# Twenty gate weight jobs as seven block products each, with branch results, gates and head outputs parked in DRAM

## The chip, the cores and the metric

The kernel runs on one core of a Trainium2 chip. Its engines are TensorE (PE, with its weight loads as PEld), VectorE (DVE), ScalarE (ACT), GpSimd (POOL) and SyncE (SP), which issues nearly all DMAs. The metric is device time in microseconds of one execution, as the median of several.

## The reference

One layer of a streaming encoder over 512 prompt tokens and 64 sample tokens (576 columns in the kernel), width 1024. One input projection feeds three branches; a gate of each branch and a merge gate come out of the same projection.

```python
xn = rms_norm(x, g_norm)
hq, hf, hi, za, dq, dk, dv, zb, mq, zm, gr = split_columns(xn @ w_in)
...
y_a = rms_norm(o_hg.transpose(0, 2, 1, 3), g_hg_out).reshape(B, T, HG_WIDTH)
...
y_b = (rms_norm(o_df, g_dsub) * (1.0 - lam_init)).reshape(B, T, DF_WIDTH)
...
y_m = memory_attention(q_m, mem_k, mem_v).reshape(B, T, MEM_WIDTH)

gates = jax.nn.sigmoid(gr).reshape(B, T, N_BRANCH, D_MODEL)
h = 0
for n, (y_n, z_n) in enumerate(((y_a, za), (y_b, zb), (y_m, zm))):
    h = h + gates[:, :, n] * ((y_n * jax.nn.silu(z_n)) @ w_branch[n])
y = x + h @ w_out
```

Branch a is a gated recurrence over 8 heads, b a differential attention over 8 heads, m an attention over 256 memory tokens with 4 heads, whose keys and values come from `rms_norm(mem_prompt) @ w_mkv`. The caches of keys, values and states are outputs too.

## The kernel before

**Arithmetic.** All products of projections are made to nearly full float32 precision from a rounded "hi" part and a "lo" remainder of each operand: hi·hi, hi·lo and lo·hi, so three matmuls for each block of 128 x 128 weights. The normalised input lies in SBUF as `xh` and `xl`, transposed. Weights come from DRAM as `raw` halves of 512 KB (`load_job`, line 163, through SP), ACT copies each quarter to `wh` (line 174), and DVE and POOL in turn make `wl` as raw minus `wh` (line 176, `lo_engine`).

**Jobs.** 76 jobs of 1024 x 256 weights each run on PE in the order of a list. A "T" job puts weights in the array and gives two blocks of 128 output channels by two halves of 288 tokens: four groups of 24 matmuls (line 213), 96 in all. An "N" job gives tokens by channels in matmuls of 256 columns (line 245): 96 over the 512 prompt tokens and 16 for the sample rows (line 257), or 48 over the 256 memory tokens. `mms` is a generator that stops after every 12 matmuls or so; at each stop `run_jobs` (line 314) converts some of the next job's weights and `weave` (line 294) takes a tick: it runs what `later` put off to this tick, and lets each active generator go one step. The work between projections (the recurrence `hgrn`, `diff_pair`, `mem_head`, the norms) is such generators, so PE's projections are the cover under which DVE, ACT and POOL do the rest. The order on each engine is this program order; nothing reorders it.

**The list.** Four recurrence pairs (hi, za, hf, hq), four jobs gr0 of branch a's merge gate, four br0 (`w_branch[0]`), the sixteen memory jobs (query, zm, key, value for each head), four gr2 and four br2, four attention pairs (dq, dk, dv, zb), four gr1 and four br1, four output jobs. The work of the last pair of each branch lies under the gr jobs that follow it.

**Evacuation.** A gr job's result is one Tanh on ACT per half (line 1356) into a `gates` tile. A z job adds one DVE operation per half (line 476, after ACT's line 475). A branch job multiplies the gate with PE's result and adds it to the running sum `h2` (lines 1368 to 1372), which stays in SBUF.

**The gates of the branch jobs.** Each finished head output is split at once into hi (ACT, line 459) and lo (POOL, line 462, `y_out`). The first branch job multiplies three groups over heads 0 to 5 (54 matmuls), then waits in the program until no generator is active, opens its `gate`, and does heads 6 and 7. SBUF scratch is a pool of "slots" (line 42): 33, and 14 more once the recurrence's own memory is given back.

Of the kernel before, what the change touches and what calls it, by code (L numbers as in the profile page):

```python
# [36 lines left out]
CW = 256  # L37

# [26 lines left out]
def encoder_step(ctx, tc, ins, outs):  # L65
# [10 lines left out]
    raws = pool("raws", 3)  # L76
    whls = pool("whls", 4)
# [32 lines left out]

    def sample_rows(key, w=CW, n=2, rows=HS0):

        ts = srows.setdefault(key, [])
        if len(ts) < n:
            ts.append(cst.tile([P, w], F32, name=nm("pad" + key)))
# [16 lines left out]
    NBASE = 33  # L132
    NMORE = 14
# [18 lines left out]
    class Job:  # L152
        def __init__(self, src, c0, kind, evac, name, pre=None, lhs=None):
            self.src, self.c0, self.kind, self.evac, self.name, self.pre, self.lhs = src, c0, kind, evac, name, pre, lhs
            self.raw, self.hi, self.lo, self.gate, self.last, self.up = [], None, None, None, False, False
# [7 lines left out]
    def load_job(j, parts=(0, 1)):  # L163
        for kh in parts:
            r = raws.tile([P, 4, CW], F32, tag="raw", name=nm("raw"))
            sy.dma_start(out=r, in_=j.src[:, 4 * kh : 4 * kh + 4, j.c0 : j.c0 + CW])
            j.raw.append(r)

    def conv_job(j, now=False):

        j.hi, j.lo, out = [], [], []

        def split(hi, lo, src):
            se.activation(out=hi, in_=src, func=AF.Copy)  # L174
            e = lo_engine()
            fn = lambda: e.tensor_tensor(out=lo, in0=src, in1=hi.bitcast(F32), op=ALU.subtract)  # L176
            if now:
                fn()
            else:
                later(1, fn)  # L180
        if j.kind == "T":
            def conv(blk, kh):
                if kh == 0:
                    j.hi.append(whls.tile([P, NK, P], F32R, tag="wh", name=nm("wh")))
                    j.lo.append(whls.tile([P, NK, P], F32R, tag="wl", name=nm("wl")))
                src = j.raw[kh][:, :, blk * P : (blk + 1) * P]
                split(j.hi[blk][:, 4 * kh : 4 * kh + 4, :], j.lo[blk][:, 4 * kh : 4 * kh + 4, :], src)
            for kh in range(2):
                for blk in range(2):
                    out.append(lambda blk=blk, kh=kh: conv(blk, kh))  # L190
        else:
            def conv(kh, s):
                if s == 0:
                    j.hi.append(whls.tile([P, 4, CW], F32R, tag="wh", name=nm("wh")))
                    j.lo.append(whls.tile([P, 4, CW], F32R, tag="wl", name=nm("wl")))
                src = j.raw[kh][:, 2 * s : 2 * s + 2, :]
                split(j.hi[kh][:, 2 * s : 2 * s + 2, :], j.lo[kh][:, 2 * s : 2 * s + 2, :], src)
            for kh in range(2):
                for s in range(2):
                    out.append(lambda kh=kh, s=s: conv(kh, s))  # L200
        return out

    def mms(j):

        if j.kind == "T":
            hi, lo = j.lhs()

            def group(blk, half, ps, k0, k1):
                sl = slice(half * TH, (half + 1) * TH)
                n = 3 * k0  # L210
                for k in range(k0, k1):
                    for w, x in ((j.hi, hi), (j.hi, lo), (j.lo, hi)):
                        pe.matmul(out=ps[:, 0:TH], lhsT=w[blk][:, k, :], rhs=x(k)[:, sl], start=(n == 0), stop=(n == 23))  # L213
                        n += 1
                        if n == 12:
                            yield
                if k1 == NK:
                    later(1, lambda: j.evac(blk, half, ps[:, 0:TH]))
                yield
            groups = [(blk, half) for blk in range(2) for half in range(2)]  # L220
            if j.gate:

                early = [(blk, half, dbank()) for blk, half in groups[0:3]]
                for g in early:
                    yield from group(*g, 0, 6)
                while active:
                    yield
                j.gate()
                for g in early:
                    yield from group(*g, 6, NK)  # L230
                groups = groups[3:]
            for blk, half in groups:
                yield from group(blk, half, dbank(), 0, NK)
        else:
            hi, lo, st, ntok = j.lhs()
            w = lambda ws, k: ws[k // 4][:, k % 4, :]

            def prompt(t2):
                ps = dbank()
                for t in range(2):  # L240
                    sl = slice((2 * t2 + t) * P, (2 * t2 + t + 1) * P)
                    n = 0
                    for k in range(NK):
                        for x, ww in ((hi, j.hi), (hi, j.lo), (lo, j.hi)):
                            pe.matmul(out=ps[:, t * CW : (t + 1) * CW], lhsT=x(k)[:, sl], rhs=w(ww, k), start=(n == 0), stop=(n == 23))  # L245
# [6 lines left out]
            def sample():  # L252
                ps = dbank()
                n = 0
                for k in range(NK):
                    for ww in (j.hi, j.lo):
                        pe.matmul(out=ps[:, 0:CW], lhsT=st[:, k, :], rhs=w(ww, k), start=(n == 0), stop=(n == 15))  # L257
# [11 lines left out]
            if st is not None and not j.last:  # L269
                yield from sample()  # L270

# [40 lines left out]
    jobs = []  # L312

    def run_jobs():
        n = len(jobs)
        for i, j in enumerate(jobs):
            if j.pre:
                j.pre()
            convs = deque(conv_job(jobs[i + 1])) if i + 1 < n else deque()

            def convert():
                convs.popleft()()
                if len(convs) % 2 == 0 and i + 2 < n:
                    later(1, lambda kh=1 - len(convs) // 2: load_job(jobs[i + 2], (kh,)))
            for s, _ in enumerate(mms(j)):
                if convs and (i or s >= 4) and len(jobs[i + 1].raw) > (4 - len(convs)) // 2:
                    convert()
                weave()
            while convs:
                convert()  # L330
# [125 lines left out]
    def y_out(h, tmp):  # L456

        hi, lo = yT[h] = slots.get(F32R), slots.get(F32R)
# [1114 lines left out]
```

## Time and profile before

| | |
|---|---|
| median of 3 runs | 1127.91 us (1127.91 to 1129.07) |
| the profiled execution's own time | 1130.34 us |
| its span in the trace | 1128.3 us |
| mean granted TensorE clock | 0.997 |
| PE busy, matmuls | 1110.9 us, 8925 |
| DVE busy | 624.2 us |
| ACT busy | 470.5 us |
| POOL busy | 461.3 us |
| DMA | 102.13 MB, mean 91 GB/s |

A row of the groups reads: line, engine, operation, output from inputs, tile shapes and count; then busy time, mean duration in ns, and the idle time of the engine just before, with what ended it. A row of the chain of waits or of the timeline begins with the start in us and the duration; "xN" is the number of instructions in it, and a bracket tells how long the engine had been idle and what released it. A row of the windows gives, for a stretch of time, the busy us and the instruction count of PE, PEld, DVE, ACT and POOL, then the granted clock, the DMA engines' busy share and GB/s.

### The profile page before, as it was taken

The page shows a single profiled execution, that of the slowest core. Times are in us where ns is not written, and L with a number is a line of the kernel's source. Part 1 is how long each engine was busy: PE and PEld are TensorE (multiplying, and loading weights), DVE is VectorE, ACT ScalarE, POOL GpSimd, SP SyncE. Part 2 cuts the span into 40 slices and gives each one's busy share as a digit, 9 for nine tenths or more (in the row PEclk, how much of TensorE's full clock was granted, in tenths as well). Part 3 has the DMA queues.
Part 4 walks back from the last instruction along what each step waited for, and adds up shares of the span by engine and source line. Part 5 has one row for each costly group of instructions (what it writes and reads, how often), then busy time and mean ns, then how long its engine had stood idle before and what let it go on. Part 6 is the DMA issues. An engine that isn't in the chain of part 4 may idle for free.

```text
span 1128.3 us, 22032 instructions
## 1 busy us (share of the span) xinstructions
PE 1110.9 (98%) x8925; PEld 1098.7 (97%) x8925; DVE 624.2 (55%) x1223; ACT 470.5 (42%) x1103; POOL 461.3 (41%) x590
## 2 busy tenths in 40 slices
PE   7999999999999999999999999999999998999998
PEld 6999999999999999999999999999999998999998
DVE  5459594967733345443422323578686785654531
ACT  6433333343341355444433213465565664653320
POOL 2436455555442154525221554436363563232120
PEclk9999999999999999999999999999999999999999
DMA  5322222122133245334221232414113123112242
GB/s 188 113 80 66 81 63 84 58 85 76 62 118 98 73 141 152 93 114 150 76 67 56 76 96 64 149 54 136 44 61 126 58 77 97 38 59 92 96 137 68
DMA packets 103093, 102.13 MB, mean 91 GB/s; under 512 B 4914, under 2 KB 101326, under 8 KB 102992
## 3 DMA queue, kind: packets, MB, share of 16 engines
q1 hardware_dynamic: 102988, 100.73, 28.7%
q8 instruction: 70, 1.15, 0.4%
q14 instruction: 31, 0.25, 0.1%
q10 hardware_dynamic: 4, 0.00, 0.0%
HBM read 90.49 MB, written 10.22 MB: 89 GB/s over the span
## 4 chain that ended last, share of the span: by engine, by line
PE 91%; DVE 4%; DMA 2%; POOL 1%; issue 1%; ACT 1%; SPq 0%; DVEq 0%; POOLq 0%
PE d L213 49%; PE d L245 25%; PE d L257 4%; PE abank L1023 1%; DMA raw<-in_w_in_dram 1%; PE abank L1226 1%; PE abank L1293 1%; PE abank L990 1%; PE abank L688 1%; PE abank L952 1%; PE abank L724 1%; PE abank L745 1%; PE abank L544 1%; DVE wl L176 1%; PE abank L951 1%
## 5 line engine op out<-in xcount | busy, mean ns | idle before, releaser
L176 POOL TENSOR_TENSOR wl<-raw,wh 128x512 fp32r<-128x512 f32 x152 | 208.3, 1374 | 348.4 <-ACT wh L174 347.5
L213 PE MATMUL d<-xh,wh 128*128 128x288 f32 x1024 | 310.8, 304 | 0.0
L213 PE MATMUL d<-xh,wl 128*128 128x288 f32 x1024 | 302.6, 295 | 0.0
L213 PE MATMUL d<-xl,wh 128*128 128x288 f32 x1024 | 302.5, 295 | 0.0
L245 PE MATMUL d<-wh,xh 128*128 128x256 f32 x768 | 221.9, 289 | 1.5 <-ACT xh L435 1.5
L245 PE MATMUL d<-wh,xl 128*128 128x256 f32 x768 | 218.0, 284 | 0.2 <-DVE xl L438 0.2
L174 ACT ACTIVATE wh<-raw 128x512 fp32r<-128x512 f32 x304 | 181.7, 623 | 87.1 <-PE d L213 61.7
L245 PE MATMUL d<-wl,xh 128*128 128x256 f32 x768 | 217.7, 283 | 0.0
L213 PEld LDWEIGHTS d<-xh,wh 128*128 128x128 f32 x1024 | 193.5, 189 | 1.0
L213 PEld LDWEIGHTS d<-xl,wh 128*128 128x128 f32 x1024 | 193.4, 189 | 0.4
L213 PEld LDWEIGHTS d<-xh,wl 128*128 128x128 f32 x1024 | 193.1, 189 | 0.0
L176 DVE TENSOR_TENSOR wl<-raw,wh 128x512 fp32r<-128x512 f32 x152 | 121.4, 799 | 123.2 <-ACT wh L174 121.2
L213 PE MATMUL d<-slot,wh 128*128 128x288 f32 x768 | 153.5, 296 | 0.0
L245 PEld LDWEIGHTS d<-wh,xh 128*128 128x128 f32 x768 | 147.4, 192 | 2.2 <-ACT xh L435 1.9
L245 PEld LDWEIGHTS d<-wh,xl 128*128 128x128 f32 x768 | 147.4, 192 | 0.7 <-DVE xl L438 0.7
L245 PEld LDWEIGHTS d<-wl,xh 128*128 128x128 f32 x768 | 147.6, 192 | 0.3
L213 PEld LDWEIGHTS d<-slot,wh 128*128 128x128 f32 x768 | 123.2, 188 | 0.0
L213 PE MATMUL d<-slot,wl 128*128 128x288 f32 x384 | 113.3, 295 | 0.0
L213 PEld LDWEIGHTS d<-slot,wl 128*128 128x128 f32 x384 | 72.3, 188 | 0.0
L1356 ACT ACTIVATE slot<-d 128x288 f32<-128x288 f32 x48 | 19.8, 412 | 107.0 <-PE d L213 107.0
L475 ACT ACTIVATE slot<-d 128x288 f32<-128x288 f32 x48 | 19.5, 409 | 92.8 <-PE d L213 91.0
L462 POOL TENSOR_TENSOR slot<-slot,slot 128x576 fp32r<-128x576 f32 x24 | 35.3, 1472 | 54.5 <-ACT slot L459 54.5
(283 smaller groups left out, 1853.1 us busy)
## 6 DMA issues: line engine op xcount, KB each, us to landing
raw<-in_w_in_dram SPq DMA_DIRECT2D x104, 512.0 KB
raw<-in_w_branch_dram SPq DMA_DIRECT2D x24, 512.0 KB
raw<-in_w_mkv_dram SPq DMA_DIRECT2D x16, 512.0 KB
out_dram<-slot SPq DMA_DIRECT2D x31, 256.0 KB
slot<-in_x_prompt_dram SPq DMA_DIRECT2D x16, 256.0 KB
raw<-in_w_out_dram SPq DMA_DIRECT2D x8, 512.0 KB
slot<-in_mem_prompt_dram SPq DMA_DIRECT2D x4, 256.0 KB
slot<-in_cache_mem_k_dram SPq DMA_DIRECT2D x4, 256.0 KB
```

The lines of the kernel that those rows point to most:

```text
L174: se.activation(out=hi, in_=src, func=AF.Copy)
L176: fn = lambda: e.tensor_tensor(out=lo, in0=src, in1=hi.bitcast(F32), op=ALU.subtract)
L213: pe.matmul(out=ps[:, 0:TH], lhsT=w[blk][:, k, :], rhs=x(k)[:, sl], start=(n == 0), stop=(n == 23))
L245: pe.matmul(out=ps[:, t * CW : (t + 1) * CW], lhsT=x(k)[:, sl], rhs=w(ww, k), start=(n == 0), stop=(n == 23))
L257: pe.matmul(out=ps[:, 0:CW], lhsT=st[:, k, :], rhs=w(ww, k), start=(n == 0), stop=(n == 15))
L462: ge.tensor_tensor(out=lo[:, 0:TT], in0=tmp[:, 0:TT], in1=hi[:, 0:TT].bitcast(F32), op=ALU.subtract)
L475: se.activation(out=dst, in_=ps, func=AF.Tanh, scale=0.5)
L544: pe.transpose(pt[:, c * P : (c + 1) * P], on[:, c * P : (c + 1) * P], ident)
L688: pe.matmul(out=a1[o0 : o0 + 64, (c % NT) * P + 32 * i : (c % NT) * P + 32 * i + 32], lhsT=Kb[:, c * KP + i * P + r0 : c * KP + i * P + r0 ...
L724: pe.matmul(out=a4[:, c * P : (c + 1) * P], lhsT=kET[:, c * P : (c + 1) * P], rhs=vt(c), start=True, stop=True)
L745: pe.matmul(out=ob[:, c * P : (c + 1) * P], lhsT=aS[:, c * P : (c + 1) * P], rhs=vt(c), start=True, stop=(c == 0))
L1356: se.activation(out=gates[b][:, half * TH : (half + 1) * TH], in_=ps, func=AF.Tanh, scale=0.5)
```

## The change

**Seven products.** A new job kind "S" is used for zb, zm and all gr jobs: 20 jobs. It takes the weights as 2 x 2 blocks (half of the depth by 128 channels) and the input as 2 x 2 blocks (half of the tokens by half of the depth) and forms the result from 7 block products of 12 matmuls, in the Winograd form, where a T job has 8. The sums of weights are made per job; the sums of the input, S1 to S4 with their hi and lo, once in `build_XS` during br0. za stays "T", since it runs before that. These are the weight sums and the seven products; `split` makes a hi on ACT and a lo on the engine named.

```python
            def op_t2(now):
                t1 = add("t1", part(0, 0), part(0, 1), ve)
                t2 = add("t2", sums["t1"], part(1, 1), ve)
...
                split(sums["t2"], P, None, now, ve, 1)
            def op_b21(now):
                split(part(1, 0), P, 1, now, ge)
                t4 = add("t4", sums["t2"], part(1, 0), ge)
...
            def op_t3(now):
                t3 = add("t3", part(0, 1), part(1, 1), ge)
...
                split(sums["t3"], P, None, now, ve, 1, t3)
            ops.append((i, 0, lambda now: split(part(0, 0), P, 0, now, ge)))
...
        order = (("A11", 0, 1), ("S2", 1, 1), ("A12", 0, 0), ("S3", 1, 0), ("S1", 2, 1), ("A22", 1, 0), ("S4", 2, 0))
...
            if p == 0:
                later(1, lambda ps=ps: se.activation(out=u1, in_=ps, func=AF.Copy))
            elif p == 1:
                later(1, lambda ps=ps: ve.tensor_tensor(out=u2, in0=ps, in1=u1, op=ALU.add))
            elif p == 2:
                later(1, lambda ps=ps: j.evac(0, 0, ps))
            elif p == 3:
                later(1, lambda ps=ps: ve.tensor_tensor(out=u3, in0=ps, in1=u1, op=ALU.add))
            elif p == 4:
                later(1, lambda ps=ps: finish(1, 1, c22, ps, u3, True))
            elif p == 5:
                later(1, lambda ps=ps: finish(0, 1, c21, ps, u1, False))
            else:
                later(1, lambda ps=ps: finish(1, 0, c12, ps, u2, True))
```

The second entry of `order` is the PSUM bank, the third whether the product starts a sum in it. A bank keeps adding after `u1`, `u2`, `u3` were read from it, so each of these reads comes between two products of its bank: u1 before product 2, u2 before product 3, u3 before product 5, and each `finish` before its bank's next use.

The listings below name instructions as line, operation, output from inputs and shape.

On DVE, at the third gr2 job of before (wl and raw are weight parts; L1190, L1234, L1247 and L1248 belong to the memory attention of the last head):

```order
L1300 SCALAR_TENSOR_TENSOR slot4_220_5917<-abank2_81,slot4_220_5917 128x512
L1300 SCALAR_TENSOR_TENSOR slot12_223_6022<-abank0_79,slot12_223_6022 128x512
L176 TENSOR_TENSOR wl_546_6832<-raw_539_6687,wh_545_6831 128x512
L1190 SCALAR_TENSOR_TENSOR slot13_264_6759<-abank3_82,gmq_103,slot35_262_6757 128x512
L176 TENSOR_TENSOR wl_546_6832<-raw_541_6723,wh_545_6831 128x512
L1190 SCALAR_TENSOR_TENSOR slot17_265_6760<-abank4_83,gmq_103,slot20_263_6758 128x512
L1234 TENSOR_REDUCE mx1_554_6949<-abank0_79 128x1
L176 TENSOR_TENSOR wl_558_6979<-raw_549_6859,wh_557_6978 128x512
```

On DVE, at the third gr2 job of after (L247 makes weight sums, L216 a lo, L435 and L437 finish an output block, d is a bank of the job's products, the others belong to attention heads):

```order
L247 TENSOR_TENSOR slot30_330_7425<-raw_755_7187 128x512
L247 TENSOR_TENSOR slot1_331_7427<-slot30_330_7425,raw_767_7268 128x512
L1461 TENSOR_REDUCE mx1_783_7410<-abank1_82 128x1
L435 SCALAR_TENSOR_TENSOR slot15_332_7432<-d_785_7412,slot8_189_4872 128x288
L1474 RECIPROCAL zz1_777_7356<-zz1_777_7356 128x1
L1475 TENSOR_SCALAR slot14_329_7398<-slot14_329_7398,zz1_777_7356 128x256
L1029 TENSOR_TENSOR slot20_304_6991<-slot20_304_6991,rsn256_764_7249 128x512
L216 TENSOR_TENSOR wl_787_7430<-slot1_331_7427,wh_786_7429 128x512
L437 TENSOR_TENSOR slot17_328_7376<-d_773_7324,slot9_188_4871 128x288
```

Where two subtractions per job stood on DVE, there are now two sums, four subtractions, and five operations that read a product bank, in one queue with the heads' work.

**The list.** The eight memory key and value jobs run right after the recurrence's jobs, in the place of gr0; their results go to DRAM (lines 1342 and 1357) and are loaded again for the heads (line 1367). gr0 comes after br0, gr2 is spread between the memory heads, and br2 lies inside the first attention pair, between dv and zb.

**Parking.** Head outputs 0 to 5 of each branch are stored to DRAM (line 647), loaded again one at a time, and split then (`y_splits`, line 654, ACT for hi and POOL for lo); 6 and 7 are split from SBUF. Branch results and gates go to DRAM and back (`h_store`, `h_load`, `g_store`, `g_load`, lines 1579 to 1595). The slots are 32 throughout; the recurrence's memory becomes the tile `XS`.

```python
            while h not in yF or len(slots.free) < (12 if hurry[0] == 1 else 4 if hurry[0] else NSPARE):
                yield
            tmp = yF.pop(h)
            if tmp is None:
                tmp = slots.get()
                sy.dma_start(out=tmp[:, 0:TT], in_=y_d[h])
                for _ in range(2 if hurry[0] else 4):
                    yield
```

**The branch gates.** The first job of br0, br1, br2 now multiplies as many heads as are split at that point, 4 to 6 (`y_there`), and then takes empty ticks until all eight are.

```python
-                    yield from group(*g, 0, 6)
-                while active:
+                    yield from group(*g, 0, k0)
+                while len(yT) < 8:
                     yield
```

In br0 and br1, k0 comes out as 4, so each of the three early groups has 12 matmuls, and six empty ticks follow; in br2 no empty tick is taken.

On SP, at br1 of before, only weight halves stand (raw):

```order
L166 DMA raw_943_11644<-in_w_in_dram 128x4x256
L166 DMA raw_960_11839<-in_w_branch_dram 128x4x256
L166 DMA raw_968_11905<-in_w_branch_dram 128x4x256
L166 DMA raw_981_12075<-in_w_branch_dram 128x4x256
L166 DMA raw_985_12118<-in_w_branch_dram 128x4x256
```

On SP, at br1 of after (y_ are parked head outputs, h2_ and g1_ parked branch results and gates):

```order
L662 DMA slot16_677_12904<-y_3_111 128x576
L185 DMA raw_1363_12946<-in_w_branch_dram 128x4x256
L1584 DMA slot15_682_12955<-h2_0_142 128x576
L1593 DMA slot28_683_12957<-g1_0_150 128x576
L1584 DMA slot5_684_12959<-h2_1_143 128x576
L1593 DMA slot18_685_12961<-g1_1_151 128x576
L1584 DMA slot3_686_12963<-h2_2_144 128x576
L1593 DMA slot27_687_12965<-g1_2_152 128x576
L1588 DMA g1_6_156<-slot22_672_12840 128x576
L185 DMA raw_1369_12993<-in_w_branch_dram 128x4x256
L1588 DMA g1_7_157<-slot17_676_12901 128x576
L662 DMA slot24_688_12997<-y_4_112 128x576
```

Six loads of parked results and two stores of gates now stand between the loads of head outputs 3 and 4 in this queue.

**Weights.** `load_next`, `conv_next` and `plan` take the place of `load_job` and `conv_job`: eight quarter units of converted weights, whatever the job, where there were four half units.

More of the change, by code (lines that the diff above doesn't have):

```diff
@@ L161, in lo_engine @@
         return ge if lo_n[0] % 2 == 0 else ve
[L163 to L176, printed above, removed]
+    jobs = []
@@ new lines, in encoder_step, with load_next @@
+    halves = []
+    units = []
+    ops = deque()
+    def load_next(limit):
+        n = len(halves)
+        i, kh = n // 2, n % 2
+        if i >= min(len(jobs), limit) or (n >= NRAW and halves[n - NRAW][2]):
+            return False
+        j = jobs[i]
+        r = raws.tile([P, 4, CW], F32, tag="raw", name=nm("raw"))
+        sy.dma_start(out=r, in_=j.src[:, 4 * kh : 4 * kh + 4, j.c0 : j.c0 + CW])
+        j.raw.append(r)
+        halves.append([j, kh, j.readers[kh]])
+        return True
@@ new lines, in conv_next, with plan, read, split @@
+    def conv_next(limit, now=False):
+        if not ops or ops[0][0] >= limit or len(jobs[ops[0][0]].raw) <= ops[0][1]:
+            return False
+        if len(units) >= NUNIT and not units[-NUNIT].done:
+            return False
+        ops.popleft()[2](now)
+        return True
+    def plan(i, j):
+        j.units = []
+        base = 2 * i
+        def read(kh):
+            halves[base + kh][2] -= 1
+        def split(src, width, kh, now, eng=None, wait=0, free=None):
+            u = Unit(width)
+            units.append(u)
+            j.units.append(u)
+            def fhi():
+                se.activation(out=u.hi, in_=src, func=AF.Copy)
+            def flo():
+                (eng or lo_engine()).tensor_tensor(out=u.lo, in0=src, in1=u.hi.bitcast(F32), op=ALU.subtract)
+                if free:
+                    slots.put(free)
+                if kh is not None:
+                    read(kh)
@@ L188, in conv_job @@
+            for blk in range(2):
+                for kh in range(2):
+                    ops.append((i, kh, lambda now, blk=blk, kh=kh: split(j.raw[kh][:, :, blk * P : (blk + 1) * P], P, kh, now)))
+        elif j.kind == "N":
+            j.readers = [2, 2]
             for kh in range(2):
-                for blk in range(2):
-                    out.append(lambda blk=blk, kh=kh: conv(blk, kh))
-        else:
[L192 to L200, printed above, removed]
@@ L206, in mms, with unit, done @@
+    def mms(j):
+        def unit(n):
+            while len(j.units) <= n:
+                assert conv_next(len(jobs)), (j.name, n)
+            return j.units[n]
+        def done():
+            for u in j.units:
+                u.done = True
+        if j.kind == "S":
+            yield from strassen(j, unit)
+        elif j.kind == "T":
             hi, lo = j.lhs()
@@ L1449, in end_hgrn, with y_start, y_next, y_all @@
             weave()
+        slots.put(*mT.values())
         hstack.close()
         more = ctx.enter_context(tc.tile_pool(name="more", bufs=1))
[L1452 to L1457 removed]
+        XS.append(more.tile([P, 2, 4, 4, TH], F32R, name="XS"))
+        push(build_XS(), 1.0)
+    def y_start():
+        hurry[0] = 0
+        push(y_splits(), 1.0)
+    def y_next():
+        y_free()
+        y_start()
+    js = branch_jobs(0)
     js[0].gate = end_hgrn
     seq += js
[L1461 to L1465 removed]
+    js = gr_jobs(0)
+    before(js[0], y_next)
+    seq += js
+    def y_all():
+        pass
     MA = []
+    gr = gr_jobs(2)
     for h in range(4):
@@ L1498, in encoder_step @@
     before(js[0], drain)
+    before(js[0], lambda: y_free())
     seq += js
     jobs.extend(seq)
+    for i, j in enumerate(jobs):
+        plan(i, j)
     with tc.manual_schedule():
```

399 lines of the change are left out of this document (291 added, 108 removed).

## The prediction

> **What bounds the kernel now.** I read the page's busy times and its chain first.
>
> ```profile
> PE 1110.9 (98%) x8925; PEld 1098.7 (97%) x8925; DVE 624.2 (55%) x1223; ACT 470.5 (42%) x1103; POOL 461.3 (41%) x590
> ...
> PE 91%; DVE 4%; DMA 2%; POOL 1%; issue 1%; ACT 1%; SPq 0%; DVEq 0%; POOLq 0%
> ```
>
> PE is busy for 98% of the span and carries 91% of the chain of waits. Time falls only if PE gets less to do, and rises by each wait on PE that is new. So the price of PE's work comes next, from the chain in the stages where nothing interrupts a job: one T job, one N job, and 12 matmuls of a T job.
>
> ```profile
> 1008.09 12.72 PE d L213 x96
> 1070.61 11.52 PE d L245 x96
> 942.60 1.59 PE d L213 x12
> ```
>
> A T job is 96 matmuls in 12.72 us, 132.5 ns each; 12 of them, one product, are 1.59 us. An N job is 120 ns each. The averages of DVE (55%) and POOL (41%) say little: they are spread over stages with different loads, and the windows below show that.
>
> **PE's saving.** Each of 20 jobs issues 84 matmuls for 96, of the same size (128 x 128 weights, 288 columns). 20 x 12 = 240 fewer, times 132.5 ns, is **−31.8 us**. All of it is on the path, since PE is. A seven-product job needs 84 x 132.5 ns = 11.13 us of PE.
>
> **What the seven products ask of the other engines.** The rows for their parts are the weight splits and the operations that read a PSUM bank:
>
> ```profile
> L176 DVE TENSOR_TENSOR wl<-raw,wh x152: 666/692/1955, 8.4 to 1099.5; 128x512 fp32r<-128x512 f32 x152
> L176 POOL TENSOR_TENSOR wl<-raw,wh x152: 1265/1292/2059, 9.0 to 1100.5; 128x512 fp32r<-128x512 f32 x152
> ...
> L174 ACT ACTIVATE wh<-raw 128x512 fp32r<-128x512 f32 x304 | 181.7, 623 | 87.1 <-PE d L213 61.7
> L476 DVE SCALAR_TENSOR_TENSOR slot<-slot,d 128x288 f32<-128x288 f32 x48 | 21.7, 453 | 55.6 <-ACT slot L475 55.0
> L475 ACT ACTIVATE slot<-d 128x288 f32<-128x288 f32 x48 | 19.5, 409 | 92.8 <-PE d L213 91.0
> ```
>
> DVE gets two sums and four subtractions of 128x512 (6 x 0.69 = 4.1 us) and five bank reads (5 x 0.45 = 2.3 us): 6.4 us in a job that had 2 x 0.69 = 1.4. POOL gets three subtractions and two sums, 5 x 1.29 = 6.45 us where it had 2.6. ACT gets seven copies and u1, 7 x 0.62 + 0.41 = 4.8 us for 2.5. Each is below 11.13 us, so taken engine by engine the work lies beside PE. But the rows' own spread says that they are not independent: one DVE subtraction takes 0.69 us at the median and 1.96 at most. The timeline shows when:
>
> ```profile
> 620.43 3.33 DVE L176 TENSOR_TENSOR wl<-raw,wh 128x512 fp32r<-128x512 f32 x2 [4.05 <-ACT wh L174]
> 619.96 3.26 POOL L462 TENSOR_TENSOR slot<-slot,slot 128x576 fp32r<-128x576 f32 x2 [11.21 <-ACT slot L459]
> ```
>
> Two DVE subtractions take 3.33 us, not 1.38, while POOL does two of its own from 619.96 to 623.22. When both engines work on two SBUF tiles, they take turns. So DVE's sums and subtractions and POOL's add up: 4.1 + 6.45 = 10.6 us in a PE job of 11.13, where it was 1.4 + 2.6 = 4.0 in 12.72. It fits by 0.5 us, before anything that the heads ask of POOL or DVE.
>
> The Trainium skill has this as a rule: "SBUF — State Buffer", "Who interferes with whom", says that DVE with two SBUF inputs and GpSimd reading SBUF use one port pair under an exclusive lock for a whole instruction. The trace agrees (3.33 us for two), and the rule speaks against this change; read strictly, with DVE stopped for each POOL operation, it gives the slower rival below.
>
> The path is touched where PE needs an answer within one product: u2, u3 and three finishing operations must leave DVE's queue in 1.59 us each, or the bank is not free. In front of such a read stands, at worst, one subtraction that waits for a POOL operation: 1.29 + 0.69 + 0.45 = 2.43 us, which is 0.84 late. None late is 0 for a job; two late are 1.7, so 34 us for 20 jobs. I take one late answer in every second job (0.84 / 2, rounded up to 0.45 for the gr0 jobs, whose DVE also does the gate product): 20 x 0.45 = **+9 us**, bounds 0 and 34. It lies nearer the lower end because the PE queue holds slack across jobs: eight converted units are made ahead, one job's worth.
>
> **The branch gates.** Before, PE was busy without a break at br0 (13.00 of 13 us in the last row below). After, heads are split one by one, so the first branch job starts with four. These rows are POOL's work at br0 before, its cost per head, the key's gain that moved here, and the loads' rate:
>
> ```profile
> 324.43 3.00 POOL L176 TENSOR_TENSOR wl<-raw,wh 128x512 fp32r<-128x512 f32 x2 [3.13 <-ACT wh L174]
> 327.39 1.43 POOL L462 TENSOR_TENSOR slot<-slot,slot 128x576 fp32r<-128x576 f32 x1
> ...
> L462 POOL TENSOR_TENSOR slot<-slot,slot 128x576 fp32r<-128x576 f32 x24 | 35.3, 1472 | 54.5 <-ACT slot L459 54.5
> L821 POOL TENSOR_TENSOR slot<-slot,slot 128x512 f32<-128x512 f32 x4 | 6.1, 1530 | 0.0
> ...
> 323.00:336.00 13.00, 13.00 (x101) 13.00 (x101) 3.60 (x7) 6.50 (x15) 5.47 (x6) 1.00 0.50 163
> ```
>
> From the first early product until head 7 is split, POOL has up to five heads (5 x 1.47), three weight subtractions (3 x 1.29) and at br0 one gain (1.53): 12.7 us. PE has three early groups of 12 and one product, 4 x 1.59 = 6.4 us. That leaves 6.3 us of wait if POOL starts with the gate, none if it was ahead. At br1 the queue of SP adds six loads of parked results, 6 x 295 KB = 1.77 MB, ahead of head 4: 10.9 us at the window's 163 GB/s, half that if the DMA share of 0.50 could double. So br1 lies between 0 and 10.9. br2 has its heads in time in the order of the program; I cost it at nothing, under cover of the dv job ahead of it. I take 4 us each for br0 and br1: POOL was 42% busy in the row above, so it is partly ahead, not wholly.
>
> Such a wait has a second price, which gr1 shows, where PE waited three times shortly after each other:
>
> ```profile
> 956.08 0.47 PE L952 MATMUL abank<-slot,slot 128*128 128x128 f32 x1 [2.33 <-POOL slot L894]
> ...
> 956.56 2.99 PE d L213 x12
> 960.40 2.42 PE d L213 x12
> ...
> 954.00:958.00 4.00, 1.92 (x8) 1.92 (x9) 1.52 (x6) 0.46 (x2) 2.38 (x6) 0.66 0.41 131
> 958.00:962.00 4.00, 4.00 (x19) 4.00 (x18) 1.72 (x7) 2.17 (x8) 0.00 (x0) 0.50 0.00 0
> ```
>
> After a wait of 2.33 us the granted clock is 0.66 and 0.50, and two products take 2.99 and 2.42 us instead of 1.59: 2.2 us lost. So each gate costs 4 + 2.2 = 6.2, two of them **+12.4 us**, bounds 0 and 6.3 + 10.9 + 4.4 = 21.6.
>
> The Trainium skill ("TensorE: Matmul & The Clock Gate", Part 1) has the half clock after an idle window of about 3.4 us and full clock after about 3.4 us of work. The trace differs in the first: here 2.33 us, after shorter waits, sufficed. By the rule applied to waits of less than 3.4 us, the two 2.2 would fall out of the sum, which would be 4.4 us lower.
>
> **The recurrence's last pair under the memory keys and values.** Its cover was gr0, 4 x 12.72 = 50.9 us. Now it is eight N jobs of 48 matmuls: 8 x 48 x 0.12 = 46.1.
>
> ```profile
> 260.00:307.00 47.00, 47.00 (x427) 46.53 (x426) 40.84 (x66) 14.41 (x34) 25.30 (x45) 1.00 0.23 71
> L818 DVE TENSOR_TENSOR slot<-slot,rsn 128x512 f32<-128x512 f32 x28 | 24.1, 878 | 6.3 <-POOL rsn L138 6.2
> L806 DVE TENSOR_REDUCE ssn<-slot 128x2 f32<-128x512 f32 x12 | 8.1, 678 | 0.0
> ```
>
> In that stage DVE was busy for 40.84 of 47 us. Eight jobs instead of four bring 8 more subtractions (5.5 us) and four key norms (4 x (0.88 + 0.68) = 6.2): 52.5 us of DVE over 46.1 of PE. The rest, 6.4, reaches into br0, where DVE had 3.60 us of work in 13, unless the early heads there wait for it. I take half: **+3 us**, bounds 0 and 6.4. POOL and ACT have room here (25.30 and 14.41 of 47).
>
> **At nothing.** The input sums S1 to S4 (DVE, POOL, ACT) are made under br0's PE work, where the window shows DVE and POOL below half; without that cover, gr0's second product would wait for them. Stores and loads of parked tiles move some 33 MB more (100 transfers of 295 KB and 16 of 262 KB) by DMAs off PE's path (mean 91 GB/s of the page before); only those ahead of a head at br0 and br1 are counted, above. gr2 and br2 change place without a change of work.
>
> **The sum.** −31.8 + 9 + 12.4 + 3 = −7.4 us. The profiled execution took 1130.34 us, its span being 1128.3, and would take 1122.9; the median of the runs is 2.4 us lower, 1127.91, and I forecast 1127.91 − 7.4 = **1120.5 us**. By the bounds of its terms, with none at its end, the forecast alone reaches from 1112 to 1127.
>
> **The rivals.** *All hidden* (0.15). The heads are split ahead of the gates and the answers are in time. For it: POOL was idle for 59% of the span, and DVE for 45%. Against it: six empty ticks at each gate in the program order. With only half-clock losses of 4.4 and the 3 us of the recurrence, −31.8 + 7.4 = −24.4, so 1103.5.
>
> *The gates take the gain* (0.17). POOL splits serially and, at br1, head 4 stands behind six loads: both gates cost their upper bound, 21.6. −31.8 + 21.6 + 9 + 3 = +1.8, so 1129.7. For it: the order of SP's queue. Against it: those loads are small beside the 0.50 share left free.
>
> *The turn-taking of DVE and POOL* (0.28) is the one on the other side: slower. In the 20 seven-product jobs 10.6 us of shared operations and 2.3 us of bank reads behind them are asked for within 11.13 us, with the heads' work on top, so two answers per job come late: 1.6 us per job, +32. −31.8 + 32 + 12.4 + 3 = +15.6, so 1143.5. It decides from (31.8 − 15.4) / 20 = 0.82 us per job on. For it: 3.33 us for two subtractions, and gr1, where DVE was busy for 43 of 63 us already:
>
> ```profile
> 942.00:1005.00 63.00, 59.73 (x434) 58.29 (x433) 43.16 (x101) 37.41 (x102) 19.68 (x29) 0.95 0.17 51
> ```
>
> Against it: POOL has 43 of those 63 us free, and five of DVE's operations read a bank and one tile.
>
> That the change does not do what it says is no rival: PE's program has 240 rows fewer, all in these jobs.
>
> **How the numbers follow.** My forecast has 0.40, the rivals 0.15, 0.17 and 0.28. What a measurement can tell here is about 0.2%, 2.3 us. Faster by more: 0.38 of the forecast's 0.40, all of the 0.15, a fifth of the gates' 0.17, together 0.56. Within 0.2%: 0.02, half of the gates' case, and a little of the turn-taking, 0.12. Slower: 0.32. The range runs from 1104, which leaves out half of the first rival, to 1140, which leaves out somewhat less than half of the last.
>
> **What would show it.** Right: PE's rows for 20 jobs have 84 matmuls; in the gr2 and gr1 stages the chain shows few waits of PE on DVE's sums, under 0.5 us a job; at br0 and br1 one wait of some 4 us each with the granted clock near 0.5 behind it. The slower rival would show as many waits of PE on lines 216, 247, 435, 437, 455 and 459, and DVE's subtractions well above 0.69 us. The gates' rival shows as a wait on line 668 (POOL's lo of a head) above 6 us at br0 and 10 at br1. The sum is wrong if PE waits where I put nothing: at br2, or in the first gr0 job for the input sums.

## The result, and the profile after

The changed kernel takes 1179.26 us (1175.07 to 1184.59), against 1128.49 of the kernel before on the same chip: a ratio of 1.045, 95% interval 1.040 to 1.050. It is slower, outside the range, and on the other side of the forecast. The profiled execution took 1181.03 us, its span is 1179.2.

The page's busy times and granted clock after:

```profile
span 1179.2 us, 22302 instructions
...
PE 1108.3 (94%) x8685; PEld 1084.7 (92%) x8685; DVE 775.3 (66%) x1419; ACT 525.2 (45%) x1207; POOL 571.8 (48%) x662
...
PEclk9999999999879999999999999998999999997999
```

PE has 240 instructions fewer, as forecast, and yet is busy for only 2.6 us less. Its idle time grew from 17.4 us (1128.3 − 1110.9) to 70.9. And it ran at half clock more often: 0.975 granted over the span where it was 0.997, which is 29.5 us of lost clock against 3.4. Part of that loss falls on PE's waits and costs nothing more: with PE at work the lost clock is 24.2 us, and 3.0 before. So −31.8 of matmuls, +53.5 of waits and, as the rest, +29.2 of slower matmuls (about 21 of it PE at work at half clock) make the +50.9 of the span.

Where PE waited, from the profile's view of who waited for whom (us in total, times, longest):

```profile
PE abank L1201 <- DVE slot L1190: 17.1, 10, 3.8
PE d L301 <- POOL slot L668: 11.8, 9, 5.9
PE d L301 <- ACT slot L666: 8.5, 2, 7.3
PE abank L1488 <- DVE slot L1475: 6.7, 8, 1.3
PE d L337 <- POOL wl L216: 4.8, 2, 2.9
...
PE d L449 <- DVE slot L435: 2.0, 3, 0.7
```

Line 449 is a seven-product matmul, and only 2.0 us were lost between products. Lines 1201 and 1488 are PE's work for attention and memory heads, waiting for the heads' own DVE operations; lines 301 and 337 are branch jobs waiting for a head's split, and memory jobs waiting for converted weights.

The windows give PE, PEld, DVE, ACT and POOL busy, granted clock, DMA share and GB/s for br0, br1, the memory key and value jobs, the memory heads, the last three attention pairs, and gr1, in this order:

```profile
331.50:360.06 28.56, 19.79 (x103) 18.35 (x102) 10.75 (x11) 7.72 (x15) 21.86 (x18) 0.76 0.40 132
1052.63:1083.16 30.53, 18.50 (x103) 16.40 (x102) 8.16 (x17) 8.43 (x18) 13.14 (x12) 0.78 0.60 205
262.00:331.50 69.50, 62.25 (x550) 60.35 (x549) 56.93 (x89) 29.35 (x60) 46.17 (x66) 0.95 0.54 173
445.84:632.57 186.73, 178.70 (x1361) 174.30 (x1360) 129.57 (x215) 91.87 (x204) 83.28 (x72) 0.99 0.34 109
745.24:970.65 225.41, 214.60 (x1708) 212.26 (x1706) 176.48 (x392) 134.45 (x337) 115.93 (x132) 0.97 0.25 79
970.65:1052.63 81.98, 70.34 (x496) 66.62 (x495) 67.84 (x144) 52.54 (x133) 39.65 (x43) 0.96 0.31 98
```

The first two rows are the first job of br0 and of br1 only: 28.56 and 30.53 us where the windows of before had one at 13.3.

```profile
322.70:336.00 13.30, 13.30 (x104) 13.30 (x103) 3.60 (x7) 6.60 (x15) 5.47 (x6) 1.00 0.49 159
259.91:322.70 62.79, 62.79 (x550) 62.32 (x549) 45.20 (x75) 20.97 (x49) 31.17 (x52) 1.00 0.23 72
722.89:942.36 219.47, 214.94 (x1750) 212.98 (x1748) 163.57 (x364) 132.61 (x335) 105.13 (x126) 1.00 0.26 82
942.36:1019.06 76.70, 73.43 (x540) 71.99 (x539) 47.56 (x108) 42.52 (x115) 26.10 (x36) 0.96 0.18 56
```

These stages got worse than their matmuls: the recurrence's last pair took 62.79 us and takes 69.50 with 4.8 less of projection (+11.5 net); the last three attention pairs 219.47 and 225.41 with 4.8 less (+10.7); gr1 76.70 and 81.98 with 6.4 less (+11.6). The four br0 jobs went from 51.5 to 66.6 and the four br1 jobs from 51.4 to 68.7 (stage times here and below are from the start of a stage's first matmul to that of the next stage). The four br2 jobs, 51.0 us for 51.2, and the output jobs, 57.9 for 57.9, did not.

### The profile page after: what moved, and what is told of

Read it like the earlier page. It is cut to its first block, busy times and chain, and to the rows that moved or that the text cites. A ratio compares the mean times of both kernels' runs of the same rounds, so it can differ in the third digit from the quotient of the medians.

```text
span 1179.2 us, 22302 instructions
## 1 busy us (share of the span) xinstructions
PE 1108.3 (94%) x8685; PEld 1084.7 (92%) x8685; DVE 775.3 (66%) x1419; ACT 525.2 (45%) x1207; POOL 571.8 (48%) x662
## 3 DMA queue, kind: packets, MB, share of 16 engines
q8 instruction: 68, 1.11, 0.4%
## 5 line engine op out<-in xcount | busy, mean ns | idle before, releaser
L216 POOL TENSOR_TENSOR wl<-raw,wh 128x512 fp32r<-128x512 f32 x172 | 237.9, 1385 | 314.8 <-ACT wh L213 268.3
L216 DVE TENSOR_TENSOR wl<-raw,wh 128x512 fp32r<-128x512 f32 x112 | 101.4, 906 | 64.4 <-ACT wh L213 63.3
L449 PE MATMUL d<-XS,wh 128*128 128x288 f32 x640 | 132.9, 301 | 2.0 <-DVE slot L435 2.0
L301 PE MATMUL d<-xh,wh 128*128 128x288 f32 x384 | 116.3, 303 | 0.0
L301 PE MATMUL d<-xh,wl 128*128 128x288 f32 x384 | 113.2, 295 | 0.0
L301 PE MATMUL d<-xl,wh 128*128 128x288 f32 x384 | 113.1, 294 | 0.0
L449 PEld LDWEIGHTS d<-XS,wh 128*128 128x128 f32 x640 | 102.7, 189 | 3.3 <-DVE slot L435 2.7
L216 DVE TENSOR_TENSOR wl<-slot,wh 128x512 fp32r<-128x512 f32 x80 | 73.1, 918 | 44.9 <-ACT wh L213 44.5
L449 PE MATMUL d<-XS,wl 128*128 128x288 f32 x320 | 94.6, 296 | 0.0
L213 ACT ACTIVATE wh<-slot 128x512 fp32r<-128x512 f32 x80 | 48.8, 625 | 82.5 <-POOL slot L247 43.8
L301 PEld LDWEIGHTS d<-xh,wh 128*128 128x128 f32 x384 | 72.1, 188 | 0.5
```

The lines of the kernel that those rows point to most:

```text
L213: se.activation(out=u.hi, in_=src, func=AF.Copy)
L216: (eng or lo_engine()).tensor_tensor(out=u.lo, in0=src, in1=u.hi.bitcast(F32), op=ALU.subtract)
L301: pe.matmul(out=ps[:, 0:TH], lhsT=w[:, k % 4, :], rhs=x(k)[:, sl], start=(n == 0), stop=(n == 23))
L449: pe.matmul(out=ps, lhsT=w[:, k, :], rhs=x(k), start=bool(first and n == 0), stop=(n == 11 and p == last[b]), skip_group_check=True)
```

## The experiments

**Theories.** A: the seven products' extra work (sums, splits, reads) makes the heads' own operations late on DVE, ACT and POOL. Within A, either DVE and POOL take turns (the rival of the prediction), or an instruction that waits holds up its queue. B: the parking and the new order make the heads late, whatever the products. C: the 12 matmuls that went were cover that the heads needed. Each run has the kernel before beside it on its own chip, at 1128.5 to 1129.8 us, so times from different chips compare to about 1 us; the changed kernel's own runs spread by 9.5 us. Small gains are therefore read by stage.

**All 20 jobs T again, and 7 of them (last three zb, gr1).**

```
-        ... Job(w_in, GR + n * D + c * CW, "S", evac, f"gr{n}")
+        ... Job(w_in, GR + n * D + c * CW, "T", evac, f"gr{n}", lhs=xT)
...
-        jz = gate_jobs(ZB + c0, A["z"])
+        jz = gate_jobs(ZB + c0, A["z"], "T" if hp else "S")
```

The first two lines stand for all gr jobs in the one kernel and for gr1 in the other, the last two for the second kernel; in the first, every z job is T.

> The changed kernel with all 20 seven-product jobs made T jobs again (8 products, 96 matmuls) and the input sums left out; the order of the list, the parking and the branch gates stay. Theory A, the seven products' extra DVE and POOL work makes the heads late (by the table of jobs they lost 37 us in these stages, against 31.8 saved): 1179 + 32 - 37, about 1174 us, and the losses at br0, br1 and under the memory keys stay. Theory B, the parking and the new order make the heads late and the seven products save their 31.8: about 1211 us.

Measured: 1159.41 us, ratio 1.027 (1.025 to 1.029). With 31.8 us more matmuls it is 20 us faster: A, and more than A said. Br0 (67.6 us) and the recurrence's end (67.6) keep their losses, as A said, but br1 does not.

> The changed kernel with 7 of the 20 jobs made T jobs again: the last three zb and the four gr1, those under the attention heads. Theory A (DVE and POOL work of the seven products): these stages lost 22 us and saved 11, so about 1168 us, with PE's waits on lines 1190 and 1104 much shorter. Theory B (parking and order): 11 us more PE work and nothing back, about 1190 us.

Measured: 1152.4 us, ratio 1.021 (1.019 to 1.023). Under the attention heads seven products cost about 20 us where they save 11: the last three pairs took 219.6 us for 225.4, and gr1 78.5 for 82.0, with 11 more of matmuls. In these two kernels the br1 stage took 51.7 us: the loss of 17 there had gone too, though nothing at br1 was edited. A zb or gr1 job of seven products has seven program stops, a T job eight; with the T jobs the program has all heads split before br1 needs them, and br1 has no empty stop. Its windows row with all T jobs:

```profile
1051.88:1103.53 51.65, 51.65 (x392) 51.65 (x391) 26.80 (x62) 17.58 (x40) 12.25 (x10) 1.00 0.52 177
```

**The matmuls taken away with no side work.** T jobs, in all 20 places, whose last group, one block of channels by one half of the tokens, leaves out the second half of the depth ("cut T jobs" below):

```
+                end = 12 if short and blk and half else 24
```

> The changed kernel with T jobs in all 20 places, each without its last 12 matmuls (one quarter of the depth of one block is left out): the same 84 matmuls as a seven-product job, seven stops, and none of its sums, reads and extra splits. If the missing 12 matmuls cost nothing by themselves (the loss is all in the sums): 1159 of the T version less 31.8, about 1128 us. If the heads used these 12 matmuls as cover: the attention stages shrink by less than 11 us, and br1 waits again; 1138 to 1150 us.

Measured: 1130.38 us, ratio 1.002 (1.001 to 1.003).

> The kernel before, with the same 12 matmuls left out of zm, zb and all gr jobs and nothing else changed: what 240 matmuls less are worth in the old order, with no sums and no parking. If all lies on the path: 1129 less 31.8, about 1098 us. If the heads need the cover: the jobs under heads give back part of it, 1103 to 1112 us.

Measured: 1100.1 us, ratio 0.975 (0.973 to 0.976). So 240 matmuls less are worth 29.5 us in the old order and 29.0 in the new, 2 to 3 less than their 31.8: on balance theory C falls. At br1 it holds: the cut T jobs, which have seven stops, wait there again (60.7 us for 51.7), and other stages give that back. These two runs split the +49.7 us (1179.3 − 1129.6) in three: −29.5 for the matmuls, +30.3 (1130.4 − 1100.1) for all else that is new (the list, the parking, the gates), +48.9 (1179.3 − 1130.4) for the seven products' own work. By stage the last is about 3 us in gr0, 12 under the memory heads, 13 in the last three attention pairs, 11 in gr1 and 8 at br1. The pages, with T jobs cut short and with seven products, have the same 8685 matmuls; this is the first:

```profile
PE 1090.8 (97%) x8685; PEld 1074.5 (95%) x8685; DVE 623.2 (55%) x1223; ACT 476.7 (42%) x1119; POOL 460.1 (41%) x590
```

DVE has 152 us less, POOL 112, ACT 48.

**What of that work.** First the sums left out, then all eleven two-tile operations on DVE.

```
-                t1 = add("t1", part(0, 0), part(0, 1), ve)
-                t2 = add("t2", sums["t1"], part(1, 1), ve)
...
+                split(part(0, 1), P, 0, now, ve)
```

> The changed kernel without the four sums of weights per seven-product job (2 operations less on DVE and 2 on POOL; the splits read the raw weights, so what the products mean is left out); everything else stays. If the turn-taking of DVE and POOL on two-tile operations makes the heads late: 80 of 220 such operations go, the shared time per job falls from 10.6 to 6.6 us, and most of the 37 us lost in these stages goes, 1145 to 1155 us. If it is the five bank reads and their place in the queue, or the parking: over 1170 us.

Measured: 1154.72 us, ratio 1.022 (1.021 to 1.024); the last three attention pairs took 208.8 us, not 225.4, but the memory heads still 183.8 for 186.7.

```
-                split(part(1, 0), P, 1, now, ge)
-                t4 = add("t4", sums["t2"], part(1, 0), ge)
+                split(part(1, 0), P, 1, now, ve)
+                t4 = add("t4", sums["t2"], part(1, 0), ve)
...
```

> The changed kernel with all eleven two-tile operations of a seven-product job on DVE; POOL gets none of them (DVE then has 11 x 0.69 = 7.6 us of them per job where it had 4.1, POOL 0 where it had 6.45). If the turn-taking of the two engines makes the heads late: 7.6 us of shared time per job for 10.6, faster than the changed kernel, 1160 to 1170 us. If the length of DVE's own queue does: 70 us more work on the engine that the heads wait for, slower, over 1190 us.

Measured: 1160.08 us, ratio 1.027 (1.025 to 1.029). More work on the loaded engine, and 19 us faster. That fits the turn-taking. But it fits something else too, which the timeline of the changed kernel shows before PE's wait of 3.81 us: two rows of POOL, one of ACT, two of DVE, one of PE.

```profile
789.85 2.91 POOL L140 TENSOR_TENSOR rsn<-rsn,nhalf 128x16 f32<-128x16 f32 x1
792.73 1.30 POOL L247 TENSOR_TENSOR slot<-raw,raw 128x512 f32<-128x512 f32 x1
...
794.06 0.63 ACT L213 ACTIVATE wh<-slot 128x512 fp32r<-128x512 f32 x1 [5.00 <-POOL slot L247]
...
788.20 0.67 DVE L733 TENSOR_TENSOR slot<-abank,rz 128x512 f32<-128x512 f32 x1
794.73 0.69 DVE L216 TENSOR_TENSOR wl<-slot,wh 128x512 fp32r<-128x512 f32 x1 [5.85 <-ACT wh L213]
...
797.34 0.47 PE L1201 MATMUL abank<-ident,slot 128*128 128x128 f32 x1 [3.81 <-DVE slot L1190]
```

A sum on POOL stands behind a head's power operation of 2.91 us. ACT's copy of the sum waits for it 5.00 us, DVE's subtraction waits for the copy 5.85 us; behind both, in order, stand the heads' exponentials and maxima. DVE stood idle there; it took no turns with anybody. The same rows stand ahead of PE's waits of 3.51 and 3.49 us in the next two pairs, where ACT waits 4.72 us for the sum. Two runs tell the two apart: the two POOL sums alone to DVE, and the three POOL subtractions alone to DVE.

> The changed kernel with all four sums of weights on DVE (two were on POOL); the three subtractions on POOL stay there. Shared two-tile time per job by the rows: 8 x 0.69 + 3 x 1.29 = 9.4 us, where it was 10.6, and 7.6 with everything on DVE (1160 us). If turn-taking was the loss: 1.2 / 3.0 of the 19 us, about 1171. If the loss was the chain of queues (ACT's copy of a sum waits for POOL, where the sum stands behind a head's rstd, and DVE's subtraction and all the heads' work behind it wait for ACT): POOL leaves the chain, and nearly all of the 19 us come, 1158 to 1164.

Measured: 1162.9 us, ratio 1.030 (1.028 to 1.032).

> The changed kernel with the seven subtractions on DVE (three were on POOL); the two sums on POOL stay there. Shared time 9 x 0.69 + 2 x 1.29 = 8.8 us per job. If turn-taking was the loss: 1.8 / 3.0 of the 19 us, about 1168. If the chain of queues through POOL's sums was: it stays, 1176 or more.

Measured: 1175.22 us, ratio 1.040 (1.037 to 1.042). The attention stage in both, sums moved and subtractions moved:

```profile
740.12:951.74 211.62, 209.50 (x1707) 207.42 (x1706) 179.93 (x399) 134.94 (x339) 107.86 (x124) 1.00 0.27 85
...
738.68:964.71 226.03, 214.72 (x1708) 211.85 (x1706) 184.00 (x403) 135.02 (x340) 102.54 (x121) 0.98 0.26 81
```

The chain of queues is the cause there: 13.8 us go with two operations per job, and none with three others that, by the rows' durations, relieve the turn-taking more. PE's waits on line 1201 in these pairs, 10.8 us in the changed kernel, are 2.1 with the sums moved and 10.3 with the subtractions moved. Under the memory heads both edits help a little (183.1 and 181.3 us for 186.7), and there the turn-taking can have a part: DVE's subtractions took 1.11 us on average, 0.73 with cut T jobs, and 0.77 with everything on DVE, where the stage took 179.7. No run takes it away alone. In gr1 neither edit helps (85.0 and 85.5 us for 82.0). In all the subtractions' edit gained 4 us, within the spread of the runs.

**The branch gates.** Loads issued a head earlier and parked results loaded later; heads 4 and 5 not parked; splits begun four jobs earlier.

```
+                if j.mid:
+                    j.mid()
...
+            if hurry[0] and yF.get(h + 1, 0) is None and len(slots.free) >= 6:
+                got[h + 1] = slots.get()
```

The other two edits are `if h < 4:` for `if h < 6:` in `y_out`, and `before(js[1], y_hurry)` for `before(js[5], y_hurry)`.

> The changed kernel with two changes at the branch gates: the load of the next parked head is issued before the split of the present one, and the six loads of parked results and gates at br1 and br2 stand behind the early groups, not ahead. If the gates wait for the loads one after the other (the latency of a load, and the queue of SP): idle time of br0 and br1 falls from 8.8 and 12.0 us to about 4 each and some of the half clock goes, 1160 to 1170 us. If they wait for POOL's splits one after the other: no change beyond 3 us, 1176 or more.

Measured: 1168.58 us, ratio 1.035 (1.033 to 1.037): br0 59.6 us and br1 59.8, but gr1 3.9 more.

> The changed kernel with head outputs 4 and 5 kept in SBUF and split from there; only 0 to 3 are parked. If the branch gates wait for the loads of heads 4 and 5: br0 and br1 lose about 3 us each instead of 15 and 17, 1155 to 1162 us. If they wait for POOL and the program's order of the splits: 1175 or more.

Measured: 1176.81 us, ratio 1.041 (1.039 to 1.043): br0 62.4 and br1 60.9, gr1 5.7 more.

> The changed kernel with the splits of the recurrence's heads begun four jobs earlier (the test of free slots relaxed from the second memory job on, not the sixth): br0's first groups run over six heads and no empty stop follows. If br0 waits because the splits come late in the program: its loss falls from 15 to some 5 us, 1167 to 1171 us. If it waits for POOL and for the last head itself: no change beyond 3 us.

Measured: 1174.48 us, ratio 1.041 (1.039 to 1.043): br0 55.8, the memory key and value jobs ahead of it 6.0 more. Each edit takes a part of the gates' loss, and part of that comes back in the stage ahead. The timeline of the changed kernel at br0 shows why no single one does: SP's loads of heads 4 and 5, their splits on ACT and POOL, and PE's waits.

```profile
337.64 0.53 SPq L662 DMA_DIRECT2D slot<-y  x1
342.82 0.33 SPq L662 DMA_DIRECT2D slot<-y  x1
...
341.85 0.69 ACT L666 ACTIVATE slot<-slot 128x576 fp32r<-128x576 f32 x1 [4.11 <-DMA slot<-y]
...
346.82 1.83 ACT L666 ACTIVATE slot<-slot 128x576 fp32r<-128x576 f32 x3 [3.77 <-DMA slot<-y]
...
337.00 1.84 POOL L668 TENSOR_TENSOR slot<-slot,slot 128x576 fp32r<-128x576 f32 x1
...
347.58 4.17 POOL L668 TENSOR_TENSOR slot<-slot,slot 128x576 fp32r<-128x576 f32 x3 [1.80 <-ACT slot L666]
...
338.90 0.61 PE L301 MATMUL d<-slot,wh 128*128 128x288 f32 x1 [5.91 <-POOL slot L668]
347.56 0.40 PE L301 MATMUL d<-slot,wh 128*128 128x288 f32 x1 [1.19 <-ACT slot L666]
349.05 0.61 PE L301 MATMUL d<-slot,wh 128*128 128x288 f32 x1 [1.09 <-POOL slot L668]
```

The first wait is for head 3, late in POOL's queue before the gate; then one load after the other, each some 4 us; then three splits in a row. At br1 the longest wait, 7.32 us, is for head 4, whose load stands behind the six loads of parked results and lands 7 us after its issue:

```profile
1059.38 0.64 SPq L662 DMA_DIRECT2D slot<-y  x1
...
1066.45 0.68 ACT L666 ACTIVATE slot<-slot 128x576 fp32r<-128x576 f32 x1 [7.38 <-DMA slot<-y]
```

**The recurrence's end.**

```
+            if j.name in ("mk", "mv"):
+                u.lo = u.hi
```

> The changed kernel in which the eight memory key and value jobs make no lo part of their weights (the products that would read it read the hi part again, so the lo part is left out of these outputs): 16 subtractions less on DVE and 16 on POOL in this stage. If the conversions, asked for at twice the rate under a job of 48 matmuls, delay PE there: the 11.5 us that the stage lost go, and the heads of br0 come earlier, 1160 to 1168 us. If the recurrence's own chain or the memory keys' norms do: no change beyond 3 us.

Measured: 1166.7 us, ratio 1.033 (1.031 to 1.034). The stage, with PE busy throughout:

```profile
262.17:319.59 57.42, 57.42 (x551) 56.98 (x549) 39.39 (x73) 29.34 (x60) 25.88 (x50) 1.00 0.65 209
```

All 11.5 us go with the lo parts: eight jobs of 48 matmuls ask for conversions at twice the rate of four jobs of 96.

**The old end of the recurrence, and a version that beats both.** gr0 as T jobs and br0 as before; memory jobs after the first memory query; seven products for zm, gr2 and the first zb.

```
+        if direct[0]:
+            hi, lo = yT[h] = slots.get(F32R), slots.get(F32R)
...
-    js = [j for h in range(4) for j in mem_jobs_kv(h)]
+    js = gr_jobs(0)
     before(js[0], late.pop())
```

> Seven products for zm, gr2 and the first zb alone (9 jobs), all else T; the recurrence's end as in the kernel before (gr0 as T jobs over its last pair, head outputs split at once, br0's early groups over six heads); memory keys and values after the first memory query and gate, and parked; the rest as in the changed kernel. If the losses are those of the table of jobs (the place of the memory jobs, the parked heads at br0, seven products under the attention heads): the kernel before, less 9 x 1.59 = 14.3, plus the 8 to 11 us lost in the memory stage, 1122 to 1127 us against 1129 of before. If parking costs time by itself: 1135 or more.

Measured: 1132.26 us, ratio 1.003 (1.002 to 1.004), between the two expectations. The stages up to br0 are back at before's times; in the memory stage PE waited 6 us, in the memory key and value jobs 3.

Then all zb too, all sums and subtractions on DVE (the edit shown above), and a stop more per job (the edit shown below):

> Seven products for zm, gr2 and all four zb (12 jobs), with all their two-tile operations on DVE and none on POOL, and eight program stops per job as a T job has; the recurrence's end, br0 and gr0, and gr1 as T jobs, as in the kernel before; the first head's memory keys loaded three jobs later. If turn-taking was the loss in the memory and attention stages: 12 x 1.59 = 19 us saved against before, some 6 us for the memory jobs' parking and their place, 1114 to 1120 us against 1129. If seven products cost the heads their time whichever engine does the sums: 1129 or more.

Measured: 1135.8 us, ratio 1.006 (1.005 to 1.007), a miss: the memory stage took 166 us, where it had taken 157.

```
             yield
+            if p == 3:
+                yield
```

> The changed kernel with one more program stop in each seven-product job (eight, as a T job has), so that the heads' steps stand as far ahead of br1 in the program as before; two empty stops are left at br1, where there were six, and its first groups run over five heads. If br1 waits because the seven-product jobs have fewer stops, so that the last head comes later in the program: br1's loss falls from 17 to about 9 us, 1168 to 1173 us. If it waits for loads or POOL: no change beyond 3 us.

Measured: 1189.9 us, ratio 1.054 (1.052 to 1.056). br1 gained 8.8 us, as expected there, but the memory stage lost 8.0, gr1 6.8 and the attention pairs 5.0: with a stop more per 84 matmuls the heads' steps come sooner than DVE's queue delivers them, and PE's waits on the memory heads' DVE operation (line 1475 in the changed kernel) grew from 5.9 to 13.6 us. With the cut T jobs this splits br1's loss: 68.7 us with seven stops and the seven products' work, 59.9 with eight stops and that work, 60.7 with seven stops and none of it, 51.7 with eight stops and none. The missing stop costs about 9 us there, the work about 8.

> The changed kernel with both edits: all two-tile operations of seven-product jobs on DVE (19 us by itself) and eight stops per job. If the two losses are separate, they add: 1150 to 1154 us. If the stops only space out the same late work: 1158 or more.

Measured: 1175.74 us, ratio 1.041 (1.040 to 1.043), a miss too, for the same reason: the same waits are 12.6 us.

The last edit, against the version of 12 jobs above:

```
-            if p == 3:
+            if p == 3 and j.name == "z" and j.c0 < MQ:
                 yield
```

> The combined kernel again, seven products in 12 jobs with all sums on DVE, but the eighth program stop only in zb; zm and gr2 have seven. If a stop more per 84 matmuls asks for the heads' steps faster than PE covers them (the memory stage took 166 us with eight stops and 157 with seven): the memory stage falls to about 151, the attention stage stays at 216, 1117 to 1121 us. If the stops do not matter and the sums on DVE slow the memory heads: 1133 or more.

Measured: 1124.76 us, ratio 0.995 (0.994 to 0.997): faster than both kernels, by 0.46% against before, and short of the 1117 to 1121 expected. Its page:

```profile
PE 1094.8 (98%) x8781; PEld 1077.7 (96%) x8781; DVE 750.6 (67%) x1407; ACT 502.6 (45%) x1159; POOL 458.0 (41%) x578
```

The memory stage fell to 154.3 us, and PE's waits on the heads' DVE operation there from 10.7 to 2.0; 12 jobs save 19 us of matmuls and keep 4.8.

## Why the prediction was wrong

**PE's saving: right.** −31.8 forecast, −29.5 measured with the same matmuls left out of the kernel before.

**The seven products: the step that failed.** "The path is touched where PE needs an answer within one product": it is not. Those waits came to 2.0 us. The cost is 48.9 us, against 9 forecast and bounds of 0 to 34, and it falls on the heads, whose instructions stand behind the jobs' in three queues; no term of the sum was for that. I added up what each engine has to do and what two of them share, and did not follow the chain sum, copy, subtraction through queues that run in order. Of the 48.9, some 13 are that chain in the attention pairs, shown by moving two sums. Of the 12 under the memory heads 3 go with the sums left out and 7 with everything on DVE, and 8 are br1's; how the work makes them is not shown in full. The 11 in gr1 go when the jobs are T jobs, and not with the sums left out, nor with all of them on DVE; what in it is the cause stays open. In that window PE waits 10.2 us for DVE's operations of the last pair, and DVE is busy for 67.84 of 81.98 us, where it was 47.56 of 76.70.

**The turn-taking rival: the right side, in the main the wrong mechanism.** At 1143.5 us it was nearest to the result, but it too made PE wait between products, and its sign hardly came: PE waited 2.0 us on line 435, and not at all on lines 247, 437, 455 and 459. The edit that should relieve it (subtractions to DVE) gained 4 us, and the edit that takes POOL's sums out of the chain 16. DVE's subtractions did stretch, to 0.91 us on average from 0.80; under the memory heads that may be a part of the loss, in the attention pairs it is not. The rule of the Trainium skill ("SBUF — State Buffer", "Who interferes with whom") holds in the rows: in the kernel before, two subtractions of 0.69 us took 3.33 beside POOL's.

**The gates: right place, too small.** 12.4 forecast, 15.1 + 17.3 = 32.4 measured, beyond the bound of 21.6. Idle time was 8.8 and 12.0 us where I took 4, above the bounds of 6.3 and 10.9; slower matmuls at half clock were 6.5 and 5.2 us where I took 2.2 from one earlier place. And br1's share hangs on the seven-product jobs: with T jobs it is 0.3. About 9 of it is their missing program stop, which the sum has no term for, and about 8 is part of the 48.9 above.

**The recurrence's last pair: right place, too small, and half of the cause.** +3 forecast, bound 6.4, measured 11.5. I counted DVE alone and let its surplus reach into br0. In truth PE waits within the stage: 4.8 us for POOL's subtractions of the next job's weights, 0.7 for DVE's, 1.7 for a step of the recurrence on POOL; and it runs 6.8 us at half clock behind that. POOL, which I said had room, was busy for 46.17 of 69.50 us.

**At nothing: right** for the input sums (no wait of gr0 on them) and for br2 (no wait). No run takes the traffic away by itself; the order of SP's queue was one part of the gates.

## What to carry to other kernels

A product saved on the bounding engine pays only if the other engines' extra instructions do not stand ahead of work that this engine waits for. Follow each new chain (here sum on POOL, copy on ACT, subtraction on DVE) through the queues in program order, and ask at each wait what stands behind it; a sum on the engine that needs it can be cheaper than one on a less busy engine. Price the saving first by leaving the work out: two runs here, with the two kernels, gave the saving, the cost of the new order and the cost of the new work apart.

## What the runs showed of the hardware

In the changed kernel's record of the granted clock there are ten stretches at 0.50 before the last instructions: five of 3.41 us, four of 6.83 and one of 13.65, all multiples of 3.41. A single wait of 1.91 us in a memory job is followed by one:

```profile
474.70:478.10 3.40, 3.40 (x18) 3.40 (x18) 3.37 (x8) 0.45 (x2) 0.02 (x1) 0.50 0.52 159
1065.00:1079.00 14.00, 8.36 (x29) 7.00 (x30) 1.60 (x4) 3.48 (x6) 6.72 (x5) 0.51 0.51 188
```

The second row is br1, where the clock stayed at half for 13.65 us while PE waited four more times between the splits, for 0.3 to 2.6 us. Of the eleven waits of PE over 1.8 us (after the start) ten have a stretch at half clock that begins before their end or at most 1.4 us after it; one of 2.86 us has none. Of the eight waits of 0.9 to 1.6 us only two, one after the other at br0, have one. So a wait of PE of about 2 us or more costs its length and, in most cases here, 1.7 us or more on top. In sum PE at work lost 24.2 us to half clock, 3.0 before: two fifths of the slowdown. The Trainium skill ("TensorE: Matmul & The Clock Gate", Part 1) gives 3.4 us of work for the way back to full clock, and the shortest stretches agree; it gives about 3.4 us of idle time as the trigger, and here 1.91 us sufficed.
